# The scale of the SSD norm kept in DRAM and applied when six groups' tiles are loaded back

## The chip, the cores and the metric

The kernel runs on one core of a Trainium2 chip. Its time is device microseconds; of several executions the median counts. A profile is one further execution, recorded by the hardware. The engines are named PE (TensorE, matmuls), DVE (VectorE), ACT (ScalarE), POOL (GpSimd) and SP (SyncE), which here issues every DMA on one queue, in program order.

## What is computed

One encoder layer for two requests of 256 tokens (together 512 columns), width 1024, all in float32. What matters here is the middle part: three branches are made from the same projection, gated, added and projected. Branch B is the state-space scan (SSD) in 8 groups of 256 channels, whose output passes a gate and an RMS norm by group. Cut to these lines:

```
u = rms_norm(x, mix_norm);  proj = u @ w_in          # q, k, v, z, xbc, dt, gate_logits
o_na  = neighborhood_attention(q_na, k_na, v_na, na_rpb)
y_ssd = (y_fwd + y_bwd + ssd_d * xs).reshape(bsz, t, D_INNER) * silu(z)
o_ssd = grouped_rms_norm(y_ssd, ssd_norm, SSD_GROUPS)  # rms over the 256 channels of a group
o_mem = memory_attention(q_m, k_m, v_m)
merged = g_na * (o_na @ w_br_na) + g_ssd * (o_ssd @ w_br_ssd) + g_mem * (o_mem @ w_br_mem)
x = x + merged @ w_out
```

The norm of a group multiplies each channel by its own weight (`ssd_norm`) and each token by one over the root of the mean square of the group's 256 channels in that token.

## The kernel before

**Layout and precision.** Activations lie with channels on the 128 partitions and the 512 tokens along the row, so a tile is 128x512. Each operand of a large product is split into a high and a low part; a product of two is three matmuls (L543 `uh,wh`, L544 `ul,wh`, L545 `uh,wl`). One call of `unit` makes one 128x512 output in a PSUM bank from eight input tiles: 24 matmuls. Such units, one after the other through the whole program, are most of what PE does.

**Weights.** `fetch` (L288) loads weights into a ring of nine buffers `wr`; `ahead` splits them two units before their use, the high part by a copy on ACT (`wh`, L320), the low part by a subtraction on DVE (`wl`, L234).

**Order.** `run` goes through a fixed plan of slots. A slot is one unit, and after it `evacuate` moves the unit before from its bank and `step` advances side tasks, which are generators: each `next` runs a task to its next `yield`. At most three or four tasks are active; `later` queues one with the tasks that must be done before it. `require` steps the tasks without units until the named ones are done. A tile framework then gives out buffers, adds the waits and orders each engine's queue. Every engine runs its queue in order. Small DVE operations can be put on a chain (`link`), from which one is taken after each large DVE operation.

**The SSD stage.** For each of the eight groups the plan has eight slots (convolution inputs, gates, the other branch's products, two `z` products). Beside them runs `t_ssd(g)`: it transposes the group's two input tiles `xs` (on PE, `xT`, L1217), makes the products `CB`, and then goes through ten steps for its eight heads. For a head it loads a broadcast row (`rw<-scr_r`, L1202), makes two decay tiles `e` (ACT, then DVE: L245 and L234), and PE multiplies them (`y`, L1278). The result, times gate, is written over `xs`, which the profile calls `cv`; `yq` is its square. After the steps PE sums the squares over the channels (`sum`, L504), and a chain of eleven small DVE operations (L270 to L276) makes the inverse root `r`, four numbers on each of 128 partitions. For the multiplication `r` must become a row that is the same on all partitions. For g < KEEP (6) this goes through DRAM: store `scr_n` (L1299), broadcast load `rw` (L1302, 256 KB), two scalings `cv<-cv,half,rw` (L1311, in the profile under the helper's line L245), and stores of the two tiles to `scr_o` (L1313). For groups 6 and 7 it is made on chip: `dg` (DVE, L512), a matmul `R` (L521), then the same scaling with `R`, and the tiles stay.

**After it.** The gates' eight units for the SSD branch follow (their tanh, `tg`, is on ACT and frees their bank), then the branch's units, each of which reads all sixteen tiles split as `osh` and `osl`. `t_os(g)` makes these: it loads `or<-scr_o` (L1322) for groups 0 to 5 and splits (ACT `osh` L256, DVE `osl` L234). Groups 0 to 3 are queued with the first gate unit, groups 4 to 7 at the branch.

Of the kernel before, what the change touches and what calls it, by code (L numbers as in the profile page):

```python
# [10 lines left out]
ALU = mybir.AluOpType  # L11
# [167 lines left out]
KEEP, EARLY, PG, LEND = 6, 4, 54, 4  # L179
# [3 lines left out]
class Layer:  # L183
# [1021 lines left out]
    def t_ssd(self, g):  # L1205
# [3 lines left out]
        rw = {n: self.rows(g, *heads[n]) for n in range(2)}  # L1209
        xs = [self.o.pop(("cv", 2 * g + i)) for i in range(2)]  # L1210
        bm, cm = self.o.pop(("cv", 16 + g)), self.o.pop(("cv", 24 + g))
        xt = []
        for i in range(2):
            ps = self.bank("xT")
# [10 lines left out]
        for b in range(2):  # L1225
            ps = self.bank("CB")
# [41 lines left out]
        for n in range(10):  # L1268
            if n < 6:
                rw[n + 2] = self.rows(g, *heads[n + 2])  # L1270
            if n >= 3 and n % 2:
                i, b, _ = heads[n - 3]
# [12 lines left out]
            if n in (5, 9):  # L1285
                v = xs[i]
# [7 lines left out]
        self.tt(y[0], y[0], y[1], ALU.add)  # L1294
        r = self.rsqrt(self.rows_to_cols(y[0])[:, 0:4], 4, 1.0 / 1024)
        if g < KEEP:
            yield
            self.link(99)
            self.nc.sync.dma_start(out=self.scr_n[g].rearrange("t p -> p t"), in_=r)  # L1299
            ps = self.g(p="rw")  # L1300
            sn = self.scr_n
            self.nc.sync.dma_start(out=ps, in_=bass.AP(sn.tensor, sn.offset + g * 512, [[0, 128], [1, 512]]))  # L1302
            yield
            yield
        else:
            dg = self.spread(r)
            yield
            ps = self.spread_mm(dg)
        for i in range(2):
            v = xs[i]  # L1310
            self.stt(v, v, self.half[:, 2 * g + i:2 * g + i + 1], ps, ALU.mult, ALU.mult)  # L1311
            if g < KEEP:
                self.nc.sync.dma_start(out=self.scr_o[2 * g + i], in_=v)  # L1313
            else:
                self.oraw[2 * g + i] = v

    def t_os(self, g):
        for k in (2 * g, 2 * g + 1):
            t = self.oraw.pop(k, None)
            if t is None:  # L1320
                t = self.g(p="or")
                self.nc.sync.dma_start(out=t, in_=self.scr_o[k])  # L1322
            self.os[k] = self.split_tile(t, "os")
        return
        yield
# [90 lines left out]
```

## Time and profile before

| | us |
|---|---|
| median of 3 runs | 1781.8 |
| lowest and highest of them | 1779.09, 1783.22 |
| the profiled execution, its own time | 1783.05 |
| span of its instructions | 1781.2 |
| busy PE, DVE, ACT in it | 1750.0, 1230.8, 848.0 |
| mean granted TensorE clock | 0.995 of full |

The span is from the first to the last instruction; what the time has beside it, 1.85 us, lies around. Positions such as 1220.02 are microseconds from the span's start. The profile's waits give, for each engine, how long it was idle just before an instruction and what ended that.

### The profile page before, as it was taken

The numbers are of one execution on the slowest core, as the hardware profiler recorded it, in microseconds if no ns is written. First come the engines' busy times: TensorE is split into PE (matmuls) and PEld (weight loads), VectorE is DVE, ScalarE is ACT, GpSimd is POOL, SyncE is SP. The second block draws the span as 40 slices with busy tenths as digits, with TensorE's granted clock in tenths as the row PEclk, the third lists the DMA queues.
The fourth block names the chain that finished last, engine by engine and source line by source line (L and its number), as shares of the span: only waits on it lengthen the run. The fifth ranks groups of instructions, "written<-read, shape, count | busy, mean of one in ns | idle before, by whom it ended". The sixth has DMA issues, their size and how long they took to land.

```text
span 1781.2 us, 22578 instructions
## 1 busy us (share of the span) xinstructions
PE 1750.0 (98%) x8568; PEld 1426.1 (80%) x8568; DVE 1230.8 (69%) x2056; ACT 848.0 (48%) x1515; POOL 0.7 (0%) x5
## 2 busy tenths in 40 slices
PE   9999999999999999999999999998999999999999
PEld 7888888888788878788877777776788878888887
DVE  7676777875645467736878777987753697776775
ACT  6443444543324335533666565666632464444442
POOL 0000000000000000000000000000000000000000
PEclk9999999999999999999999999999999999999999
DMA  6134324542323132333333443446434324343331
GB/s 256 64 134 142 108 93 136 166 142 95 95 74 118 60 114 80 116 95 95 127 105 137 128 128 103 145 136 177 142 113 136 95 95 131 94 142 129 91 124 47
DMA packets 79708, 209.69 MB, mean 118 GB/s; under 512 B 11120, under 2 KB 19696, under 8 KB 79600
## 3 DMA queue, kind: packets, MB, share of 16 engines
q1 hardware_dynamic: 79600, 208.26, 36.7%
q8 instruction: 67, 1.10, 0.2%
q14 instruction: 41, 0.34, 0.1%
HBM read 198.64 MB, written 9.58 MB: 117 GB/s over the span
## 4 chain that ended last, share of the span: by engine, by line
PE 84%; DVE 7%; DMA 5%; issue 1%; ACT 1%; SPq 0%; DVEq 0%; ACTq 0%
PE ac L565 21%; PE m L543 9%; PE m L545 9%; PE m L544 9%; PE q L587 5%; PE q L589 5%; PE q L588 5%; PE d L544 4%; PE d L545 4%; PE d L543 4%; DMA scr_n<-y 3%; DVE cv L245 2%; DVE wl L234 2%; DMA rw<-scr_r 2%; PE y L1278 1%; DVE e L245 1%
## 5 line engine op out<-in xcount | busy, mean ns | idle before, releaser
L320 ACT CAST wh<-wr 128x1024 fp32r<-128x1024 f32 (+1 forms) x357 | 371.0, 1040 | 681.2 <-PE ac L565 166.8
L234 DVE TENSOR_TENSOR wl<-wr,wh 128x1024 fp32r<-128x1024 f32 (+1 forms) x357 | 431.4, 1209 | 270.5 <-ACT wh L320 265.3
L543 PE MATMUL m<-uh,wh 128*128 128x512 f32 (+1 forms) x584 | 236.3, 405 | 1.4 <-ACT tg L249 1.4
L565 PE MATMUL ac<-wh,sh 128*128 128x512 f32 (+1 forms) x616 | 229.3, 373 | 0.8 <-ACT wh L320 0.8
L545 PE MATMUL m<-uh,wl 128*128 128x512 f32 (+1 forms) x584 | 229.5, 393 | 0.0
L544 PE MATMUL m<-ul,wh 128*128 128x512 f32 (+1 forms) x584 | 229.4, 393 | 0.0
L565 PE MATMUL ac<-wl,sh 128*128 128x512 f32 (+1 forms) x616 | 228.1, 370 | 0.7 <-DVE wl L234 0.7
L565 PE MATMUL ac<-wh,sl 128*128 128x512 f32 (+1 forms) x616 | 228.1, 370 | 0.0
L543 PEld LDWEIGHTS m<-uh,wh 128*128 128x128 f32 (+1 forms) x584 | 110.2, 189 | 35.8 <-issue 8.4
L544 PE MATMUL d<-hl,wh 128*128 128x512 f32 x352 | 137.2, 390 | 0.7 <-DVE hl L234 0.7
L543 PE MATMUL d<-hh,wh 128*128 128x512 f32 x352 | 137.4, 390 | 0.5 <-ACT hh L256 0.5
L545 PE MATMUL d<-hh,wl 128*128 128x512 f32 x352 | 137.0, 389 | 0.0
L565 PEld LDWEIGHTS ac<-wh,sh 128*128 128x128 f32 x616 | 116.0, 188 | 21.0 <-ACT wh L320 1.7
L565 PEld LDWEIGHTS ac<-wl,sh 128*128 128x128 f32 x616 | 116.1, 189 | 20.7 <-DVE wl L234 1.2
L565 PEld LDWEIGHTS ac<-wh,sl 128*128 128x128 f32 x616 | 116.0, 188 | 19.6
L545 PEld LDWEIGHTS m<-uh,wl 128*128 128x128 f32 (+1 forms) x584 | 109.9, 188 | 26.0 <-issue 1.5
L544 PEld LDWEIGHTS m<-ul,wh 128*128 128x128 f32 (+1 forms) x584 | 110.2, 189 | 21.9
L249 ACT ACTIVATE e<-rw,lots 128x256 f32<-128x256 f32 (+1 forms) x256 | 97.8, 444 | 46.3 <-DMA rw<-scr_r 46.3
L245 DVE SCALAR_TENSOR_TENSOR x<-d,x 128x512 f32<-128x512 f32 x96 | 66.2, 690 | 77.1 <-PE d L545 76.8
L587 PE MATMUL q<-wh,uh 128*128 128x512 f32 x256 | 102.5, 400 | 0.0
L234 DVE TENSOR_TENSOR wr<-wr,wr 128x1024 f32<-128x1024 f32 x80 | 97.6, 1221 | 5.6 <-DMA wr<-in_w 4.3
L588 PE MATMUL q<-wh,ul 128*128 128x512 f32 x256 | 100.3, 392 | 0.0
(253 smaller groups left out, 2868.1 us busy)
## 6 DMA issues: line engine op xcount, KB each, us to landing
wr<-in_w SPq DMA_DIRECT2D x308, 512.0 KB
rw<-scr_r SPq DMA_DIRECT2D x64, 256.0 KB
nv<-scr_v SPq DMA_DIRECT2D x64, 64.0 KB
scr_o<-cv SPq DMA_DIRECT2D x12, 256.0 KB
or<-scr_o SPq DMA_DIRECT2D x12, 256.0 KB
wr<-in_w SPq DMA_DIRECT2D x9, 256.0 KB
x<-in_xT SPq DMA_DIRECT2D x8, 256.0 KB
mr<-in_memT SPq DMA_DIRECT2D x8, 256.0 KB
```

The lines of the kernel that those rows point to most:

```text
L234: self.V.tensor_tensor(out=out, in0=a, in1=b, op=op)
L245: self.V.scalar_tensor_tensor(out=out, in0=a, scalar=s, in1=b, op0=op0, op1=op1)
L249: self.S.activation(out=out, in_=x, func=f, **kw)
L320: self.S.copy(hi[:, :n], t[:, :n])
L543: self.T.matmul(ps[:m], wh[:, kk, :], xh, start=i == 0, stop=False)
L544: self.T.matmul(ps[:m], wh[:, kk, :], xl, start=False, stop=False)
L545: self.T.matmul(ps[:m], wl[:, kk, :], xh, start=False, stop=i == n - 1)
L565: go = lambda l, r, **f: self.T.matmul(ps, l, r, skip_group_check=True, **f)
L587: self.T.matmul(self.qb[t], xh, wh[:, kk, :], start=k == 0, stop=False)
L588: self.T.matmul(self.qb[t], xl, wh[:, kk, :], start=False, stop=False)
L589: self.T.matmul(self.qb[t], xh, wl[:, kk, :], start=False, stop=k == KD - 1)
L1278: T.matmul(yb[64 * hp:64 * hp + 64, b * 256:(b + 1) * 256], xt[i][:, (2 * b + st) * 128 + 64 * hp:(2 * b + st) * 128 + 64 * hp + 64], w[hp ...
```

## The change

The scale `r` of groups 0 to 5 stays in DRAM. `t_ssd` stores its two tiles unscaled to `scr_o` before the norm is made, then stores `r` to `scr_n` and ends, two `yield`s earlier than before. `t_os` loads `r` as a broadcast row together with the tiles and scales each tile after its load, ahead of the split. Groups 6 and 7 are as before. The number of DMAs and of DVE operations stays the same.

```
         if g < KEEP:
+            for i in range(2):
+                self.nc.sync.dma_start(out=self.scr_o[2 * g + i], in_=xs[i])
             yield
             self.link(99)
             self.nc.sync.dma_start(out=self.scr_n[g].rearrange("t p -> p t"), in_=r)
-            ps = self.g(p="rw")
-            sn = self.scr_n
-            self.nc.sync.dma_start(out=ps, in_=bass.AP(sn.tensor, sn.offset + g * 512, [[0, 128], [1, 512]]))
-            yield
-            yield
-        else:
-            dg = self.spread(r)
-            yield
-            ps = self.spread_mm(dg)
+            return
+        dg = self.spread(r)
+        yield
+        ps = self.spread_mm(dg)
         for i in range(2):
-            v = xs[i]
-            self.stt(v, v, self.half[:, 2 * g + i:2 * g + i + 1], ps, ALU.mult, ALU.mult)
-            if g < KEEP:
-                self.nc.sync.dma_start(out=self.scr_o[2 * g + i], in_=v)
-            else:
-                self.oraw[2 * g + i] = v
+            self.scale_o(g, i, xs[i], ps)
+            self.oraw[2 * g + i] = xs[i]
+
+    def scale_o(self, g, i, v, r):
+        self.stt(v, v, self.half[:, 2 * g + i:2 * g + i + 1], r, ALU.mult, ALU.mult)
 
     def t_os(self, g):
-        for k in (2 * g, 2 * g + 1):
+        if g < KEEP:
+            r, sn = self.g(p="rw"), self.scr_n
+            self.nc.sync.dma_start(out=r, in_=bass.AP(sn.tensor, sn.offset + g * 512, [[0, 128], [1, 512]]))
+        for i in range(2):
+            k = 2 * g + i
             t = self.oraw.pop(k, None)
             if t is None:
                 t = self.g(p="or")
                 self.nc.sync.dma_start(out=t, in_=self.scr_o[k])
+                self.scale_o(g, i, t, r)
             self.os[k] = self.split_tile(t, "os")
```

What this does to the engines' queues is shown at three places. Numbers behind a name tell one buffer from another; they differ between the kernels.

**First piece: PE, the end of group 7,** just ahead of the SSD branch's first unit. In the kernel before, `sum` stands inside a gate unit `m_11108`, whose matmuls are the three lines of a product:

```order
L543 MATMUL m_11108<-uh_3254,wh_11000 128x512
L544 MATMUL m_11108<-ul_3255,wh_11000 128x512
L545 MATMUL m_11108<-uh_3254,wl_11001 128x512
L543 MATMUL m_11108<-uh_3261,wh_11000 128x512
L504 MATMUL sum_11077<-consts,yq_10932 128x1 x4
L544 MATMUL m_11108<-ul_3262,wh_11000 128x512
L545 MATMUL m_11108<-uh_3261,wl_11001 128x512
L543 MATMUL m_11108<-uh_3320,wh_11000 128x512
```

and `R` eleven matmuls later:

```order
L543 MATMUL m_11108<-uh_3381,wh_11000 128x512
L544 MATMUL m_11108<-ul_3382,wh_11000 128x512
L545 MATMUL m_11108<-uh_3381,wl_11001 128x512
L521 MATMUL R_11101<-dg_11085,consts 128x128 x4
L543 MATMUL m_11108<-uh_3388,wh_11000 128x512
L544 MATMUL m_11108<-ul_3389,wh_11000 128x512
```

In the changed kernel the last `y` of group 7 is followed by the same two:

```order
L545 MATMUL m_11035<-uh_3381,wl_10930 128x512
L543 MATMUL m_11035<-uh_3388,wh_10929 128x512
L544 MATMUL m_11035<-ul_3389,wh_10929 128x512
L1278 MATMUL y_10972<-e_10982,xt_10546 64x256
L1278 MATMUL y_10972<-e_10965,xt_10546 64x256
L1278 MATMUL y_10972<-e_10982,xt_10546 64x256
L545 MATMUL m_11035<-uh_3388,wl_10930 128x512
L504 MATMUL sum_11069<-consts,yq_10924 128x1 x4
L521 MATMUL R_11093<-dg_11077,consts 128x128 x4
L543 MATMUL m_11100<-uh_3206,wh_10992 128x512
L544 MATMUL m_11100<-ul_3207,wh_10992 128x512
L545 MATMUL m_11100<-uh_3206,wl_10993 128x512
```

The last `y` stands six matmuls later in its unit than before (seven of that unit follow it there, one here), and `sum` and `R` have moved up ahead of the next unit, next to each other.

**Second piece: SP, the norm of group 0.** Before (`cv_7052` and `cv_7125` are the group's tiles, `rw<-scr_r` loads those of the group behind it):

```order
L1299 DMA scr_n<-y_7844 128x4x1
L1302 DMA rw_7913<-scr_n 128x512
L1202 DMA rw_7915<-scr_r 128x512
L1202 DMA rw_7967<-scr_r 128x512
L288 DMA wr_8049<-in_w 128x1024
L1202 DMA rw_8026<-scr_r 128x512
L1313 DMA scr_o<-cv_7052 128x512
L1313 DMA scr_o<-cv_7125 128x512
L288 DMA wr_8113<-in_w 128x1024
```

and in the changed kernel:

```order
L1298 DMA scr_o<-cv_7125 128x512
L1202 DMA rw_7783<-scr_r 128x512
L1202 DMA rw_7848<-scr_r 128x512
L1202 DMA rw_7915<-scr_r 128x512
L1202 DMA rw_7967<-scr_r 128x512
L288 DMA wr_7935<-in_w 128x1024
L1202 DMA rw_8022<-scr_r 128x512
L288 DMA wr_7983<-in_w 128x1024
L1301 DMA scr_n<-y_7844 128x4x1
L288 DMA wr_8045<-in_w 128x1024
L288 DMA wr_8109<-in_w 128x1024
```

The load behind the store is gone, the loads `rw<-scr_r` that stood behind it are ahead of it, and the tile's store too.

**Third piece: ACT and DVE at the place of the first.** ACT before:

```order
L320 CAST wh_11046<-wr_10577 128x1024
L256 CAST osh_10824<-or_10822 128x512
L256 CAST osh_10831<-or_10829 128x512
L320 CAST wh_11111<-wr_10579 128x1024
L249 ACTIVATE tg_10895<-m_10717 128x512
L249 ACTIVATE tg_10965<-m_10864 128x512
L249 ACTIVATE tg_11028<-m_10934 128x512
L249 ACTIVATE yq_11041<-cv_10473 128x512
L249 ACTIVATE tg_11074<-m_10997 128x512
```

and in the changed kernel:

```order
L320 CAST wh_11038<-wr_10553 128x1024
L256 CAST osh_10802<-or_10798 128x512
L320 CAST wh_11103<-wr_10555 128x1024
L256 CAST osh_10810<-or_10807 128x512
L249 ACTIVATE yq_11033<-cv_10453 128x512
L256 CAST osh_10819<-or_10816 128x512
L256 CAST osh_10826<-or_10823 128x512
L249 ACTIVATE tg_10887<-m_10693 128x512
L249 ACTIVATE tg_10957<-m_10856 128x512
```

`tg`, the tanh whose unit's bank the next unit takes, stands ahead of `yq` before; now it stands behind two copies `osh`, and these need scaled tiles `or`. DVE, from the last `y` to the scaling by `R`, before:

```order
L245 SCALAR_TENSOR_TENSOR cv_10473<-cv_10473,half,y_10980 128x512
L234 TENSOR_TENSOR cv_10473<-cv_10473,zt_10677 128x512
L234 TENSOR_TENSOR osl_10832<-or_10829,osh_10831 128x512
L234 TENSOR_TENSOR wl_11112<-wr_10579,wh_11111 128x1024
L234 TENSOR_TENSOR yq_10932<-yq_10932,yq_11041 128x512
L270 TENSOR_SCALAR v_11082<-sum_11077 128x4
```

and in the changed kernel:

```order
L245 SCALAR_TENSOR_TENSOR cv_10453<-cv_10453,half,y_10972 128x512
L245 SCALAR_TENSOR_TENSOR or_10807<-or_10807,half,rw_10796 128x512
L234 TENSOR_TENSOR cv_10453<-cv_10453,zt_10653 128x512
L234 TENSOR_TENSOR wl_11104<-wr_10555,wh_11103 128x1024
L234 TENSOR_TENSOR osl_10811<-or_10807,osh_10810 128x512
L234 TENSOR_TENSOR yq_10924<-yq_10924,yq_11033 128x512
L270 TENSOR_SCALAR v_11074<-sum_11069 128x4
```

A scaling of `or` has come between the result of `y` and the add of the squares `yq`, and `wl` and `osl` have changed places. Farther on in the changed kernel, the end of the inverse root:

```order
L275 SCALAR_TENSOR_TENSOR t_11076<-t_11076,v_11074 128x4
L276 SCALAR_TENSOR_TENSOR y_11075<-t_11076,y_11075 128x4
L234 TENSOR_TENSOR osl_10820<-or_10816,osh_10819 128x512
L512 TENSOR_SCALAR dg_11077<-consts,y_11075 128x128 x4
L245 SCALAR_TENSOR_TENSOR cv_10340<-cv_10340,half,R_11093 128x512
L245 SCALAR_TENSOR_TENSOR or_10823<-or_10823,half,rw_10814 128x512
L245 SCALAR_TENSOR_TENSOR cv_10453<-cv_10453,half,R_11093 128x512
L234 TENSOR_TENSOR osl_10827<-or_10823,osh_10826 128x512
```

Here an `osl` stands ahead of `dg`, and the scaling of the second `or` between the two by `R`; a scaling of `or` stands inside the inverse root as well. Before, nothing stands there.

## Rows read from the trace of the kernel before

**Rows 1.** The page's first part: the span, then each engine's busy time, its share of the span, and its instructions.

```profile
span 1781.2 us, 22578 instructions
PE 1750.0 (98%) x8568; PEld 1426.1 (80%) x8568; DVE 1230.8 (69%) x2056; ACT 848.0 (48%) x1515; POOL 0.7 (0%) x5
```

**Rows 2.** The waits of PE over the whole span: the waiting instruction, what it waited for, us in total, times, the longest.

```profile
PE y L1278 <- DVE e L234: 7.6, 5, 5.2
PE xT L1217 <- DVE cv L245: 7.0, 4, 2.2
...
PE m L543 <- ACT tg L249: 1.4, 1, 1.4
```

**Rows 3.** The same view of SP's DMA queue, of DVE and of ACT, the rows that touch the change.

```profile
SPq L1302 <- DMA scr_n<-y: 48.8, 6, 8.8
...
DVE cv L245 <- DMA rw<-scr_n: 34.2, 6, 6.8
...
ACT e L249 <- DMA rw<-scr_r: 46.3, 6, 8.6
...
ACT osh L256 <- DMA or<-scr_o: 4.3, 4, 1.4
```

**Rows 4.** The timeline of SP's queue in group 5: start, duration, line, transfer.

```profile
1210.38 0.38 SPq L1299 DMA_DIRECT2D scr_n<-y  x1
...
1220.02 0.33 SPq L1302 DMA_DIRECT2D rw<-scr_n  x1
```

**Rows 5.** The timelines of DVE, ACT and PE at the same place; in brackets the idle time before and what ended it.

```profile
1224.07 0.75 DVE L245 SCALAR_TENSOR_TENSOR cv<-cv,half,rw 128x512 f32<-128x512 f32 x1 [5.61 <-DMA rw<-scr_n]
...
1226.04 1.49 ACT L249 ACTIVATE e<-rw,lots 128x256 f32<-128x256 f32 x4 [7.70 <-DMA rw<-scr_r]
...
1219.75 0.40 PE L545 MATMUL m<-uh,wl 128*128 128x512 f32 x1
1225.31 1.94 PE L1278 MATMUL y<-e,xt 128*64 128x256 f32 x6 [5.16 <-DVE e L234]
```

**Rows 6.** Busy time by stretch: from and to, length, then busy time and count of PE, PEld, DVE, ACT, POOL, the granted clock, the DMA engines' share and GB/s. First periods of the SSD groups, from one store of `scr_n` to the next; then two stretches behind waits; last the end of the stage.

```profile
930.80:985.10 54.30, 53.68 (x249) 41.10 (x248) 45.52 (x95) 35.41 (x74) 0.00 (x0) 1.00 0.39 131
985.10:1041.80 56.70, 54.76 (x250) 42.26 (x249) 45.57 (x96) 35.47 (x74) 0.00 (x0) 0.97 0.41 126
...
1154.90:1210.40 55.50, 53.89 (x250) 41.12 (x249) 45.58 (x95) 35.47 (x74) 0.00 (x0) 1.00 0.42 128
...
1002.70:1006.00 3.30, 3.30 (x11) 2.73 (x11) 3.30 (x8) 2.38 (x5) 0.00 (x0) 0.50 0.26 99
...
1225.30:1231.20 5.90, 5.89 (x16) 3.93 (x17) 5.90 (x12) 5.08 (x12) 0.00 (x0) 0.50 1.04 395
...
1262.00:1285.00 23.00, 23.00 (x108) 15.47 (x107) 18.89 (x41) 15.63 (x36) 0.00 (x0) 1.00 0.54 182
```

**Rows 7.** The timeline of PE at the end of group 7. Instructions of one form that follow each other are one row.

```profile
1287.10 0.50 PE L543 MATMUL m<-uh,wh 128*128 128x512 f32 x1 [1.40 <-ACT tg L249]
...
1287.90 0.40 PE L543 MATMUL m<-uh,wh 128*128 128x512 f32 x1
...
1289.27 0.39 PE L543 MATMUL m<-uh,wh 128*128 128x512 f32 x1
1289.50 0.95 PE L504 MATMUL sum<-consts,yq 128*128 128x1 f32 x8
1290.31 0.48 PE L544 MATMUL m<-ul,wh 128*128 128x512 f32 x1
...
1292.67 0.39 PE L545 MATMUL m<-uh,wl 128*128 128x512 f32 x1
1293.09 1.13 PE L521 MATMUL R<-dg,consts 128*128 128x128 f32 x8
1293.98 0.47 PE L543 MATMUL m<-uh,wh 128*128 128x512 f32 x1
```

**Rows 8.** The timeline of DVE at the same place, the first `y` result to the scaling by `R`.

```profile
1283.91 0.75 DVE L245 SCALAR_TENSOR_TENSOR cv<-cv,half,y 128x512 f32<-128x512 f32 x1 [2.53 <-PE y L1278]
1284.69 0.69 DVE L234 TENSOR_TENSOR cv<-cv,zt 128x512 f32<-128x512 f32 x1
1285.30 0.69 DVE L234 TENSOR_TENSOR osl<-or,osh 128x512 fp32r<-128x512 f32 x1
1286.59 1.23 DVE L234 TENSOR_TENSOR wl<-wr,wh 128x1024 fp32r<-128x1024 f32 x1 [0.60 <-ACT wh L320]
1288.58 0.69 DVE L234 TENSOR_TENSOR yq<-yq,yq 128x512 f32<-128x512 f32 x1 [0.77 <-ACT yq L249]
1290.48 0.16 DVE L270 TENSOR_SCALAR v<-sum 128x4 f32<-128x4 f32 x1 [1.21 <-PE sum L504]
...
1292.66 0.88 DVE L512 TENSOR_SCALAR dg<-consts,y 128x128 f32<-128x128 f32 x4
1294.26 1.41 DVE L245 SCALAR_TENSOR_TENSOR cv<-cv,half,R 128x512 f32<-128x512 f32 x2 [0.73 <-PE R L521]
```

**Rows 9.** Groups of instructions by line, engine, operation and form: count, busy us, mean ns of one, idle time before.

```profile
L245 DVE SCALAR_TENSOR_TENSOR cv<-cv,half,rw 128x512 f32<-128x512 f32 x12 | 8.6, 750 | 34.2 <-DMA rw<-scr_n 34.2
...
L249 ACT ACTIVATE tg<-m 128x512 f32<-128x512 f32 x24 | 13.8, 591 | 0.0
L256 ACT CAST osh<-or 128x512 fp32r<-128x512 f32 x12 | 7.3, 616 | 4.3 <-DMA or<-scr_o 4.3
```

## The prediction

> **What bounds the kernel now.** I read the page's engine shares first: PE is busy 1750.0 of 1781.2 us [rows 1]. PE takes its instructions in order, so only what leaves a hole in PE, or lowers its clock, costs time, and a change elsewhere is worth what it does to those holes. Then PE's waits [rows 2]: of few that there are, the first two belong to the SSD stage, `y` behind DVE's `e` 7.6 us and `xT` behind DVE's `cv` 7.0 us. They name DVE, which is only 69% busy [rows 1], so something holds DVE up. The waits of the other engines [rows 3] tell what: DVE's scaling of `cv` waits 34.2 us in six times for the load `rw<-scr_n`; SP, which issues every DMA in order, waits 48.8 us in six times for the store `scr_n<-y` to land before it can issue that load; and ACT waits 46.3 us for `rw<-scr_r`, loads of the next group that stand in SP's queue behind it. The last group with this store shows the chain on one clock [rows 4, 5]: the store is issued at 1210.38 and the load only at 1220.02; DVE starts its scaling at 1224.07 after 5.61 us idle, ACT starts at 1226.04 after 7.70, and PE, which left its last matmul at 1219.75, starts `y` at 1225.31. So PE's 14.6 us in this stage are the round trip through DRAM, passed on by two in-order queues.
>
> **The change, part by part: what it takes away.** In groups 0 to 5 nothing in the SSD stage reads `scr_n` any more: the load and the scaling go to `t_os`. The store stays and nothing waits for it for a long time, so SP goes on at once to `wr` loads, while the next `rw<-scr_r` loads stand ahead of it (second piece of order). The terms:
> - PE's waits: 7.6 + 7.0 = 14.6 us [rows 2].
> - A hole costs more than its idle time, since the pipeline drains: from 1219.75 to 1225.31 [rows 5] is 5.56 us, 5.33 above the pitch of 0.23 between `m` matmuls (six from 1287.90 to 1289.27, [rows 7]), against 5.16 shown as idle. Nine holes at 0.2 make 1.8 us.
> - Clock: after two of the holes the granted clock is 0.50, the 1.2 GHz level, for 3.30 and 5.90 us with PE busy throughout [rows 6]. Half of each is lost: 1.65 + 2.95 = 4.6 us.
>
> The gain is 14.6 + 1.8 + 4.6 = 21.0 us. A check from other rows: the first group's period, with one hole of 0.6, is 54.3 us; the four that follow last 1210.4 - 985.1 = 225.3 us, 8.1 above four times that [rows 6]. They hold the 7.0 of `xT`, no more of `y` than the first, and the 1.65 of the clock, 8.65 in all: the holes do carry through to the end. What the freed stage does with its time must not be a new hole: DVE is busy 45.5 of 54 to 57 us a group [rows 6], and loses the two scalings (1.5 us at 750 ns, [rows 9]), so it has 8 us a group to spare. The `scr_o` stores are issued earlier, behind a DVE row that is due anyway; I cost them at nothing, covered by the three to eight `wr` buffers ahead, and if that cover were gone each could delay a weight load by the wait for its tile. Bounds of the gain: 14.6 (waits alone, the clock falling elsewhere) and 21.6 (0.3 a hole).
>
> **What it adds.** Twelve scalings `or<-or,half,rw` (0.75 us each, 9.0 us on DVE) and six loads go to the stretch before the SSD branch. DVE is busy there 18.89 of 23.00 us [rows 6], so the five scalings that fall ahead of the last `y` (3.5 us at 0.70) about fill it. That is DVE time, not PE time. But the tail's order on PE changes, and this is the dear part (first piece of order). Before, seventeen matmuls stand between the last `y` and `sum`, and eleven more ahead of `R`; they cover DVE's chain. Now `sum` and `R` follow the last `y` with one matmul between, back to back, so PE stands through the whole of it. And the next unit's first matmul waits for a tanh `tg` to free its bank (it does so before, 1.40 us, [rows 2, 7]), which on ACT now stands behind two `osh` copies, the second of which wants a scaling that stands behind `R` (third piece).
>
> The chain from the start of DVE's `cv<-cv,half,y`, durations from [rows 8, 9]: 0.78 to the next start, scaling of `or` 0.70, `cv,zt` 0.61, `wl` 1.23, `osl` 0.61, `yq` add 0.69: 4.6. From the add's end (1288.58 + 0.69) to `v` at 1290.48: 1.21, makes 5.8. The eleven small operations to `dg`, 1290.48 to 1292.66: 2.18, makes 8.0. A scaling and an `osl` set among them: 1.4, makes 9.4. `dg` to the scaling by `R`, 1292.66 to 1294.26: 1.60, makes 11.0. That scaling 0.70, the second `or` 0.75, `osh` 0.62, `tg` 0.59: 13.7 us. The chain starts in before's time at 1283.91 plus six matmuls by which the last `y` now stands later (1.4) plus 0.5 for a DVE that is full: 1285.8. So the next unit starts at 1299.5 where it started at 1287.10 [rows 7]: 12.4 us later. `sum` and `R` are then behind it already; before, they took 0.58 (1289.50 to 1290.31, less a pitch) and 1.08 (1292.67 to 1293.98, less one): 1.66. That leaves 10.7. After a hole of 5.16 us the clock cost 2.95; I take 3.0 for this one too. Loss 13.7 us. Its bounds: 8 (no clock loss, the slip nothing, `tg` not held by the last `osh`) and 20 (3 us of slip on a full DVE, 6.8 us at half clock, `sum` and `R` at the low clock too). The four scalings of groups 4 and 5, later still, stand ahead of `os` tiles that the branch's first unit reads last; I cost them at nothing, from 0 to 3 us.
>
> **Sum.** 13.7 - 21.0 = -7.3 us on the profiled execution's 1783.05, so 1775.7. That execution is 1.25 above the median of 1781.8, so for the median 1774.5.
>
> The price of a clock that has fallen is the one term that could be read otherwise. Rows 6 show 3.30 and 5.90 us at half clock behind holes of 1.94 and 5.16 us. The Trainium skill, page "TensorE: Matmul & The Clock Gate", section "HAM oscillation — how this bites in real kernels", reports about 1.67 us throttled behind each wait of its kernel, half of it lost. By that figure, as an estimate, two stretches give back 1.7 in place of 4.6 and the new one costs 0.8 in place of 3.0: -6.6 in place of -7.3. The measured stretches decide.
>
> **Rivals.**
> (a) *The tail is hidden and the gain comes whole.* For it: in before DVE's chain there is covered and PE waits 1.40. Against: PE's order leaves one matmul of cover. It gives 1783.05 - 21.0 - 1.25 = 1760.8. Chance 0.14.
> (b) *The tail eats the gain.* The clock falls as often as before, only elsewhere, so the gain is the waits, 14.6, and the tail costs 13.7 or a little more: 1779 to 1784. The 9.4 us of the chain ahead of `dg` are on a DVE that has no slack, which speaks for it. Chance 0.16.
> (c) *Slower: the scalings stand on DVE waiting for their loads.* Before, only ACT's copy waits for `or<-scr_o`, 4.3 us in four times [rows 3], while DVE goes on. Now DVE, in order, waits for `or` and `rw`, and behind it stand the `e` that PE's `y` need. From its issue at 1220.02 a load is used at 1224.07: 4.05 us [rows 4, 5]. Four of the eight tiles exposed by that are 16.2 us, less the 4.1 idle on DVE (23.00 - 18.89): 12.1 more on PE, net +4.8, 1786.6. It decides from a tail loss of 21.0 + 3.6 = 24.6 us on, three to four loads wholly exposed. Against it: the loads are issued well ahead where buffers are free. Chance 0.12.
> (d) *The holes stay.* PE's `y` waits name DVE's `e`, not the load; if DVE is late there by its own work, 2.4 of them remain and the result is 1777. It lies inside my forecast's own range.
>
> **The numbers.** My forecast (net -3.6 to -15) has 0.58; its own range is 1766 to 1778. Bounds of both terms, -21.6 + 8 and -14.6 + 20, reach from 1768 to 1787. 0.2% of this time is 3.6 us, about what a measurement can tell from no change, so faster means under 1778.2 and slower over 1785.4. Faster is my forecast and (a), 0.72; same is (b), 0.16; slower is (c), 0.12. The range 1763 to 1783 leaves out most of (a) below and (c) above, 2 in 10.
>
> **What would show it.** The gain is right if DVE has no wait for `rw<-scr_n` in the SSD groups, SP none of 8 us there, PE's `xT` waits are gone, the group period is 53 to 54 us, and the clock stays at 1.00 to the end of group 5. The tail is right if PE waits for `sum`, `R` and `m` in a row for some 10 us just ahead of the SSD branch, with the clock at 0.50 behind it. I am wrong if DVE's waits for `or<-scr_o` or the moved `rw<-scr_n` reach 10 us, if PE's `y` waits for `e` grow in groups 6 and 7, or if the group period stays at 56.

## The result and the profile after

The changed kernel takes 1768.5 us, median of 4 runs (1767.54 to 1769.75), against 1782.5 for the kernel before in the same comparison (4 runs, 1779.09 to 1784.56). The ratio is 0.9924, interval 0.9907 to 0.9941, so 10.5 to 16.6 us are saved. The forecast was faster, 1774.5 in a range of 1763 to 1783: the direction and the mechanism held, and the saving came out at 14 us where 7 were forecast. The profiled execution took 1768.09 us with a span of 1766.3.

The page's first part of the changed kernel, to be read against [rows 1]:

```profile
span 1766.3 us, 22623 instructions
...
PE 1741.1 (99%) x8568; PEld 1425.2 (81%) x8568; DVE 1232.2 (70%) x2056; ACT 847.3 (48%) x1515; POOL 0.7 (0%) x5
```

PE's busy time has fallen by 8.9 us with the same number of instructions, so part of what was lost before had counted as busy. PE's waits over the whole span, against [rows 2]:

```profile
PE sum L504 <- DVE yq L234: 4.1, 1, 4.1
PE R L521 <- DVE dg L512: 3.7, 1, 3.7
...
PE m L543 <- ACT tg L249: 2.7, 1, 2.7
...
PE y L1278 <- DVE e L234: 0.7, 1, 0.7
```

`xT` is off the list and `y` is down from 7.6 to 0.7. At one place the waits for `sum` and `R` are new, and the one for `tg` has grown from 1.4 to 2.7. Of DVE's and ACT's waits for these loads, against [rows 3], none for `scr_n` is left, and two remain:

```profile
DVE or L245 <- DMA or<-scr_o: 4.5, 2, 2.3
...
ACT e L249 <- DMA rw<-scr_r: 1.1, 1, 1.1
```

The periods of the SSD groups, from one store of `scr_n` to the next, and three later stretches (from and to, length, then busy time and count of PE, PEld, DVE, ACT, POOL, granted clock, DMA share, GB/s), against [rows 6]:

```profile
930.90:983.10 52.20, 52.20 (x250) 40.91 (x249) 44.64 (x93) 35.27 (x75) 0.00 (x0) 1.00 0.42 131
983.10:1035.30 52.20, 52.20 (x250) 40.90 (x249) 44.63 (x93) 35.29 (x75) 0.00 (x0) 1.00 0.53 131
...
1139.70:1191.90 52.20, 52.20 (x250) 40.91 (x249) 44.63 (x93) 35.27 (x75) 0.00 (x0) 1.00 0.45 132
...
1262.80:1272.70 9.90, 3.63 (x16) 3.28 (x16) 6.30 (x21) 1.73 (x4) 0.00 (x0) 0.50 0.36 127
1272.80:1276.30 3.50, 3.50 (x8) 2.77 (x9) 0.13 (x1) 1.86 (x4) 0.00 (x0) 0.50 0.00 0
```

A group now takes 52.2 us with PE busy all of it, where it took 54.3 to 56.7. The clock is at 1.00 through the SSD groups and at 0.50 (the 1.2 GHz level) from 1262.8 to 1276.3, behind the last `y` and a wait of 4.1 us. That place, on PE, DVE and ACT of the changed kernel, against [rows 7, 8]:

```profile
1257.08 1.08 PE L1278 MATMUL y<-e,xt 128*64 128x256 f32 x6
1258.09 0.50 PE L545 MATMUL m<-uh,wl 128*128 128x512 f32 x1
1262.69 1.70 PE L504 MATMUL sum<-consts,yq 128*128 128x1 f32 x8 [4.10 <-DVE yq L234]
1268.06 2.05 PE L521 MATMUL R<-dg,consts 128*128 128x128 f32 x8 [3.68 <-DVE dg L512]
1272.76 0.80 PE L543 MATMUL m<-uh,wh 128*128 128x512 f32 x1 [2.65 <-ACT tg L249]
...
1258.19 0.75 DVE L245 SCALAR_TENSOR_TENSOR cv<-cv,half,y 128x512 f32<-128x512 f32 x1 [1.58 <-PE y L1278]
...
1261.86 0.68 DVE L234 TENSOR_TENSOR yq<-yq,yq 128x512 f32<-128x512 f32 x1
1264.42 0.16 DVE L270 TENSOR_SCALAR v<-sum 128x4 f32<-128x4 f32 x1 [1.88 <-PE sum L504]
...
1267.64 0.87 DVE L512 TENSOR_SCALAR dg<-consts,y 128x128 f32<-128x128 f32 x4
1270.15 0.75 DVE L245 SCALAR_TENSOR_TENSOR cv<-cv,half,R 128x512 f32<-128x512 f32 x1 [1.64 <-PE R L521]
1270.81 0.75 DVE L245 SCALAR_TENSOR_TENSOR or<-or,half,rw 128x512 f32<-128x512 f32 x1
...
1271.59 0.62 ACT L256 CAST osh<-or 128x512 fp32r<-128x512 f32 x1 [4.68 <-DVE or L245]
1272.12 2.54 ACT L249 ACTIVATE tg<-m 128x512 f32<-128x512 f32 x5
```

This is the chain that was forecast, link by link: `y`, the square's add, `sum`, the inverse root, `dg`, `R`, the second scaling of `or`, `osh`, `tg`, and only then the next unit.

How far the changed kernel is ahead at each place follows from equal matmuls. The last run of `y` in the kernel before:

```profile
1282.79 1.08 PE L1278 MATMUL y<-e,xt 128*64 128x256 f32 x6
```

Its start, plus 1.4 for the six matmuls by which it now stands later, less 1257.08, is 27.1 us. The first `m` of the next unit: 1287.10 [rows 7] less 1272.76, 14.3 us. So the SSD groups gave 27 and the tail took back 13.

### The profile page after: what moved, and what is told of

Read it like the earlier page. It is cut to its first block, busy times and chain, and to the rows that moved or that the text cites. A ratio compares the mean times of both kernels' runs of the same rounds, so it can differ in the third digit from the quotient of the medians.

```text
span 1766.3 us, 22623 instructions
## 1 busy us (share of the span) xinstructions
PE 1741.1 (99%) x8568; PEld 1425.2 (81%) x8568; DVE 1232.2 (70%) x2056; ACT 847.3 (48%) x1515; POOL 0.7 (0%) x5
## 4 chain that ended last, share of the span: by engine, by line
PE 95%; DVE 3%; DMA 1%; issue 0%; ACT 0%; DVEq 0%; SPq 0%; ACTq 0%
PE ac L565 20%; PE m L543 12%; PE m L544 12%; PE m L545 12%; PE q L587 5%; PE q L589 5%; PE q L588 5%; PE d L544 5%; PE d L545 5%; PE d L543 5%; PE y L1278 2%; PE hT L690 1%; PE CB L1228 1%; DVE wl L234 1%; PE amo L875 1%; PE am L847 1%
## 5 line engine op out<-in xcount | busy, mean ns | idle before, releaser
L589 PE MATMUL q<-wl,uh 128*128 128x512 f32 x256 | 100.6, 393 | 0.0
```

The lines of the kernel that those rows point to most:

```text
L589: self.T.matmul(self.qb[t], xh, wl[:, kk, :], start=False, stop=k == KD - 1)
```

## Experiments

All times are medians of 4 runs, and ratios are to the kernel before on the same chip in the same job.

**1. Is it the round trip?** Kernel before, the load reads elsewhere:

```
             ps = self.g(p="rw")
-            sn = self.scr_n
+            sn = self.scr_r
```

> The kernel before, but the broadcast load behind the store of the scale reads a row of the decay scratch that was written long ago, so it does not wait for the store to land; the store stays, and so do the load's size, both scalings, the stores of the tiles and every yield. The scaling is by wrong numbers: the norm's scale is left out of groups 0 to 5. My theory (the round trip through DRAM is the gain): SP's 8 us waits and DVE's 34 us are gone, PE's waits for xT and y go, the tail stays covered, and the time is 24 to 28 us below the kernel before, near 1756. Rival (the gain comes from taking twelve scalings off DVE and two steps off each group's task): both are still there, so it lies within 6 us of before.

Measured: 1755.39 us, ratio 0.9852 (0.9837 to 0.9866), 26 us less. In its SSD groups PE has no wait and DVE none for `rw`, while the scalings and yields are where they were. The rival falls; the whole of the gain is there without moving the scalings. The scheduler does order PE otherwise here: its `m` matmuls are broken by runs of `y` 34 times, as in the changed kernel, and not 40 as in the kernel before. So the 26 us hold the waits and this difference of order together (run 8 prices the breaks). One of the four small `y` holes of the kernel before and two of its four `xT` holes, on PE; this kernel has none of them:

```profile
953.44 1.05 PE L1278 MATMUL y<-e,xt 128*64 128x256 f32 x6 [0.62 <-DVE e L234]
...
1002.59 1.05 PE L1217 MATMUL xT<-consts,cv 128*128 128x128 f32 x4 [1.94 <-DVE cv L245]
...
1115.90 0.63 PE L1217 MATMUL xT<-consts,cv 128*128 128x128 f32 x4 [2.21 <-DVE cv L245]
```

The `xT` at 1002.59 ran at a granted clock of 0.50 [rows 6], those at 1115.90 at 1.00.

**2. Do the two yields matter?** Changed kernel:

```
             self.nc.sync.dma_start(out=self.scr_n[g].rearrange("t p -> p t"), in_=r)
+            yield
+            yield
             return
```

> The changed kernel with the two yields of before put back behind the store of the scale, so that each group's task ends as late as before. My theory (the gain is the wait, the tail is made by the moved scalings): as the changed kernel, 1768.5 within 2 us, with the same waits for sum, R and m of 4, 4 and 3 us. Rival (ending two steps earlier makes the gain, or makes the tail): either the SSD periods grow back and it is 5 us or more slower, or the tail's waits go and it is 10 us faster.

Measured: 1768.43 us, ratio 0.9926 (0.9910 to 0.9943), and the same waits for `sum`, `R` and `tg` (4.1, 3.7, 2.6). Ending the tasks earlier makes neither the gain nor the loss.

**3. Is the tail made by the moved scalings?** Changed kernel, `t_os` without them:

```
-        if g < KEEP:
-            r, sn = self.g(p="rw"), self.scr_n
-            self.nc.sync.dma_start(out=r, in_=bass.AP(...))
...
-                self.scale_o(g, i, t, r)
```

> The changed kernel without the loads of the scale and the twelve scalings where the tiles are loaded back: the norm's scale is left out of groups 0 to 5. My theory (they alone lead to sum and R standing bare): the tail is covered as before, PE's waits for sum and R are below 1 us, and the time is 12 to 14 us below the changed kernel, near 1755. Rival (the tail's order comes from tasks that end earlier): the waits of 4, 4 and 3 us stay and the time is within 3 us of 1768.5.

Measured: 1756.08 us, ratio 0.9855 (0.9840 to 0.9869), 12.5 below the changed kernel. PE's only wait from 900 to 1330 us is that for `tg` of before:

```profile
PE m L543 <- ACT tg L249: 1.4, 1, 1.4
```

With the loads and the scalings out, `sum` and `R` stand in PE's queue as they did before, apart and covered. So the loss goes with them: with them in, the scheduler puts `sum` and `R` elsewhere. What they cost as work alone is not told apart; three scalings of `or`, some 0.7 us each, stand in the changed kernel's chain of 14.6 us.

**4. Fewer of them ahead of the branch.** Changed kernel:

```
-KEEP, EARLY, PG, LEND = 6, 4, 54, 4
+KEEP, EARLY, PG, LEND = 6, 2, 54, 4
```

> The changed kernel with only groups 0 and 1 loaded back, scaled and split during the gates, and 2 to 7 at the branch (the constant EARLY 2 in place of 4). In its order on PE, 22 rows stand between the last y and sum and 13 more ahead of R. My theory (the loss is the bare chain): the waits for sum, R and m go, unless the branch's first unit has to wait for the eight scalings that are later now; 8 to 13 us below the changed kernel, 1755 to 1760. Rival (the eight scalings at the branch cost what they saved): PE waits there for osh or osl by 5 to 10 us and the time stays within 4 us of 1768.5.

Measured: 1760.58 us, ratio 0.9882 (0.9868 to 0.9897), 8 below the changed kernel, just outside the range given. PE's waits from 1230 to 1330 us:

```profile
PE m L543 <- ACT osh L256: 2.0, 2, 1.1
PE m L543 <- ACT wh L320: 1.4, 1, 1.4
PE m L545 <- DVE wl L234: 0.4, 1, 0.4
```

The bare chain is gone and the branch's first units wait a little for their tiles. Both theories hold in part: 12 to 13 us saved at the one place and the 1.4 for `tg` with it, and by the start times of the matmuls some 6 paid at the other, of which the waits listed are 3.8.

**5. The scale on chip for all groups.** Kernel before:

```
-        if g < KEEP:
-            yield
...
-            yield
-        else:
-            dg = self.spread(r)
-            yield
-            ps = self.spread_mm(dg)
+        dg = self.spread(r)
+        yield
+        ps = self.spread_mm(dg)
```

> The kernel before with the scale of all eight groups made a row on chip, as it does for groups 6 and 7 (dg on DVE, the matmul R on PE, the scaling by R, then the stores of the tiles for groups 0 to 5): the same results, no scr_n at all. It keeps 40 runs of y matmuls between m matmuls, as before has; the changed kernel has 34. My theory (holes as they are listed, and beside them about 0.7 us for each run of y that breaks the m matmuls once more): 1781.5 less 27.5, plus six breaks or 4, plus six R of 1.1 us or 6.5: 1764 to 1765, and in the trace 29 plain runs of y between m, against 23. Rival (the breaks cost nothing, all of the 27 is the holes): 1760 to 1761, with a break at its own matmuls' time.

Measured: 1765.77 us, ratio 0.9907 (0.9893 to 0.9922). The number is near the forecast, but for another reason. From 920 us on, where the kernel before has 29 plain runs of `y` between `m`, this one has 24 runs with `y` and no `CB`, 7 of them with `R`: the count of 40 that I expected took a run broken by `R` for one broken by `m`. PE's timeline at the first of these `R`:

```profile
933.61 0.38 PE L521 MATMUL R<-dg,consts 128*128 128x128 f32 x2
933.92 0.65 PE L1278 MATMUL y<-e,xt 128*64 128x256 f32 x2
934.50 0.94 PE L521 MATMUL R<-dg,consts 128*128 128x128 f32 x6
935.37 1.08 PE L1278 MATMUL y<-e,xt 128*64 128x256 f32 x6
```

`R` costs here not the 1.1 us of [rows 7] but breaks a run of `y` in two as well. Against run 1 the time is 10 us longer, or 1.7 for each of the six. So the run shows again that no round trip means no hole, and says nothing of its own on breaks.

**6. Which queue passes the wait on?** Kernel before:

```
             self.nc.sync.dma_start(out=self.scr_n[g].rearrange("t p -> p t"), in_=r)
+            yield
+            yield
             ps = self.g(p="rw")
...
             yield
-            yield
```

> The kernel before with one more yield, two of the three between the store of the scale and the emission of its load; in SP's order the load still stands directly behind the store, the scaling comes one step later. It tells apart which in-order queue passes the round trip on. Theory A (DVE's queue: the scaling stands on it waiting): DVE's waits for rw<-scr_n fall to below 5 us and so do PE's holes, time near 1757, although SP goes on waiting 8 us six times. Theory B (SP's queue: the next group's rw<-scr_r stand behind the blocked load): ACT's waits for rw<-scr_r stay at 30 to 50 us, PE keeps waits for y, time 1766 to 1776. I expect B, with xT's waits gone and some of y's left.

Measured: 1755.42 us, ratio 0.9846 (0.9830 to 0.9863). I expected B and got A's time. SP, DVE and ACT in this kernel, against [rows 3]:

```profile
SPq L1304 <- DMA scr_n<-y: 44.2, 6, 8.1
...
DVE cv L245 <- DMA rw<-scr_n: 6.2, 6, 1.3
...
ACT e L249 <- DMA rw<-scr_r: 0.4, 1, 0.4
```

SP waits for the store as long as before (44.2 against 48.8 us), and PE has no wait in the SSD groups at all. The time is that of run 1, in which SP does not wait, so SP's blocked queue costs nothing here by itself: what cost was that DVE and ACT stood for what comes through it. In this kernel four `rw<-scr_r` stand ahead of the store:

```profile
1178.50 1.85 SPq L1202 DMA_DIRECT2D rw<-scr_r  x4
...
1193.76 0.38 SPq L1299 DMA_DIRECT2D scr_n<-y  x1
1196.53 0.33 SPq L288 DMA_DIRECT2D wr<-in_w  x1
1203.07 0.33 SPq L1304 DMA_DIRECT2D rw<-scr_n  x1
1203.44 0.42 SPq L1202 DMA_DIRECT2D rw<-scr_r  x1
```

Both the scaling and the use of the row loads have moved away from the block, so whether DVE's wait or ACT's was the dearer is not told apart.

**7. Scaled a group later.** Kernel before; `t_ssd` of the next group loads and scales:

```
         for n in range(10):
+            if late and n == 4:
+                lr, sn = self.g(p="rw"), self.scr_n
+                self.nc.sync.dma_start(out=lr, in_=bass.AP(...))
+            if late and n == 6:
+                for i in range(2):
+                    self.scale_o(late[0], i, late[1][i], lr)
+                    self.nc.sync.dma_start(out=self.scr_o[2 * late[0] + i], in_=late[1][i])
```

The stores go with the scaling; the load, the scalings and their two yields leave the group's own task, and a group's `t_os` waits for the next group's task.

> The kernel before, but a group's scale is loaded, and its tiles scaled and stored, in the steps 4 and 6 of the next group's task; on SP some ten DMAs stand between the store and the load. The same results. The twelve scalings stay in the SSD groups and t_os is as before. My theory (the round trip is the gain, the scalings among the gates are the loss): both PE's holes in the SSD stage and the tail's waits are gone, 1755 to 1758, 11 to 13 us below the changed kernel. Rival (the scalings and late stores fill DVE in the SSD groups, or the tiles come late for the gates' loads): waits of PE for e or for osh come back, 1760 or more.

Measured: 1756.14 us, ratio 0.9852 (0.9837 to 0.9867). As my theory had it: SP has no wait for the store any more, PE none but the 1.4 for `tg`. It is no faster than run 6, in which SP still waits.

**8. What does a break cost?** Kernel of run 6:

```
-                for st in range(2):
-                    for hp in range(2):
-                        T.matmul(yb[...], xt[i][...], w[hp][0][...], start=st == 0, stop=st == 1)
+                half = lambda st, i=i, b=b, w=w, yb=yb: [T.matmul(yb[...], ...) for hp in range(2)]
+                half(0)
+                if n in (5, 9):
+                    half(1)
+            elif n in (4, 8):
+                half(1)
```

> The kernel of the run with the scaling a step later, with the same y matmuls, but in every other step the second half of the four is issued one step later; so PE's m matmuls are broken by y 47 times by its order, in place of 34. Results as the reference. My theory for the part of the gain that the listed waits don't hold (the kernel before breaks them 40 times, the changed one 34): each break costs about 0.65 us beside its own matmuls, 13 more make 8.5: 1763 to 1765, with no waits of PE in the SSD stage. Rival (a break costs nothing, the 27 us were all holes): 1755 to 1757.5.

Measured: 1759.49 us, ratio 0.9865 (0.9847 to 0.9883); run 6 had 1755.42 and 0.9846, and the intervals overlap, so of the times alone neither number is settled. The trace has the price. A run of `y`, from PE's timeline of the kernel before, of the changed kernel, and of this one, with the `m` on both sides:

```profile
938.03 0.39 PE L545 MATMUL m<-onh,wl 128*128 128x512 f32 x1
938.35 0.65 PE L1278 MATMUL y<-e,xt 128*64 128x256 f32 x2
938.93 0.50 PE L543 MATMUL m<-uh,wh 128*128 128x512 f32 x1
...
939.50 0.40 PE L545 MATMUL m<-uh,wl 128*128 128x512 f32 x1
939.82 1.08 PE L1278 MATMUL y<-e,xt 128*64 128x256 f32 x6
940.83 0.50 PE L543 MATMUL m<-uh,wh 128*128 128x512 f32 x1
```

```profile
937.59 0.39 PE L545 MATMUL m<-onh,wl 128*128 128x512 f32 x1
937.91 1.08 PE L1278 MATMUL y<-e,xt 128*64 128x256 f32 x8
938.92 0.50 PE L543 MATMUL m<-uh,wh 128*128 128x512 f32 x1
```

```profile
933.72 0.39 PE L545 MATMUL m<-uh,wl 128*128 128x512 f32 x1
934.04 0.65 PE L1277 MATMUL y<-e,xt 128*64 128x256 f32 x4
934.62 0.50 PE L543 MATMUL m<-on,wh 128*128 128x512 f32 x1
```

From `m` to `m`, less the pitch of 0.23: 0.67 us for a run of two, 0.67 for four, 1.10 for six and for eight. Split into two and six, eight cost 1.77, or 0.67 more; split into four and four 1.34, or 0.24 more. The first `m` behind each run is followed after 0.34 us and not 0.23, so each run more costs another 0.11. Both theories fail on their number for this kernel: thirteen more runs, most of them even halves, cost 3.5 us from `m` to `m` and 1.4 behind them, not 8.5 and not nothing; PE's wait of 1.4 for `tg` is gone here, so that the whole is some 3.4. For the kernel before, whose six more runs are the uneven kind, the 0.67 each stands.

## Why the prediction was right, and what was mis-sized

- **The bound and the mechanism** held: the holes in PE came from the round trip and went with it (runs 1 and 3). DVE has no wait for `rw<-scr_n` in the changed kernel, the clock stays at 1.00 through the SSD groups, and the three waits of the tail stand in a row, 10.5 us in all, with the clock at 0.50 from the end of the first, much as foretold.
- **The loss** was forecast at 13.7 us; the places above give 13 (27 ahead, then 14.3, and 14.9 in the span), and taking the scalings out gave 12.5 (run 3). The chain from `cv<-cv,half,y` to the next unit took 14.57 us against 13.7, the steps being: to the end of the square's add 4.35 (4.6 forecast), to `v` 6.23 (5.8), to `dg` 9.45 (9.4), to the scaling by `R` 11.96 (11.0), to `m` 14.57. What is over is the clock: `sum` and `R` ran at half of it, 1.70 and 2.05 us in place of 0.95 and 1.13. The `m` matmuls behind the chain lost 1.8 us to it, where I took 3.0.
- **The gain was mis-sized**: 21.0 forecast, 27 measured, and that is nearly the whole of the miss. It lies outside the bounds that I gave it, 14.6 to 21.6 (the upper one is 21.9 by its own terms); the net of 14 us is near the edge of the 3.6 to 15 that I gave it. From the start times of all PE matmuls of this stretch in the kernel before and in run 1, less the pitch, it divides so.
  - `xT`: 8.1 us where 7.0 of idle was listed. 0.3 of it is four `xT` at half clock (run 1), so a hole costs 0.2 above its idle time, as I took it.
  - The `y` hole of 5.2: 6.1, of which 0.85 is its six `y` at half clock (1.94 us in place of 1.08), so that hole costs 0.1 above its idle time.
  - The four `y` holes of 0.6, 2.4 together: 4.9, twice their idle time, where I took 0.2 each.
  - The clock: 3.1 on the `m`. With the shares of `xT` and `y` it makes 4.3, against 4.6 forecast, so this term held.
  - Four `sum`: 0.7, at a granted clock of 1.00; what held them is not shown.
  - And 4.4 that I had no term for, 4.0 from `m` to `m` and 0.4 on the `m` behind: the kernel before breaks its `m` matmuls once more in each of six groups, by two and six `y` where the changed kernel has eight in one run (run 8). That was in the order of the two kernels, and I read the order only where the change moved something that I knew of. Why the scheduler breaks them there is not shown.
- **The check that I made by the periods** hid this: it compared four groups with a first one that itself holds a hole and a break. The base is 52.2 us, not 54.3.
- **Two in-order queues pass the wait on**, I wrote, and costed SP's block as part of it. Run 6 shows that SP's block, kept almost whole, costs nothing once what is needed soon stands ahead of it.
- **The throttled time.** From the end of the tail's first wait the clock is at 0.50 for 13.5 us, of which PE works some 7. The figure of 1.67 us behind each wait, from the Trainium skill's page "TensorE: Matmul & The Clock Gate" (section "HAM oscillation — how this bites in real kernels"), makes 5.0 for three waits, as an estimate, and is too small here; the measurement decides.
- **Rivals**: (a) fell by the three waits; (b) by the gain; (c) by the waits for the loads, DVE's for `or<-scr_o` are 4.5 us in all, in two; (d) by PE's `y` at 0.7.

The best version is neither kernel: the kernel before with one more step between the store and the scaling (run 6) takes 1755.4 us, 13 below the change, and leaves nothing out; run 7 is level with it.

## What to carry over

A wait that an in-order engine passes on is mended by giving the answer time to come, one step of other work between request and use; moving the use far away can cost more where it lands. Before a piece of work is moved, read the whole order of the engine that sets the time, not only at the places that the change names: here the scheduler moved two groups of short matmuls out of their cover at one end, and joined runs of short matmuls at the other. Cost a hole by the starts on both sides, not by its idle time.

## What was not expected of the hardware

- A run of short `y` matmuls between long ones costs by its break as much as by its number: 0.67 us for two or for four, 1.10 for six or for eight.
- SP stood for 44 us in six waits (run 6) and the kernel lost nothing by it: 1755.4 us against 1755.4 in run 1 and 1756.1 in run 7, where it does not wait.
- At the end of a wait of 4.1 us the granted clock fell to 0.50, and it stayed there from 1262.8 to 1276.3, through the waits of 3.7 and 2.7 us that followed and 3.5 us beyond. In the kernel before, it had fallen behind a wait of 1.94 us, and not behind one of 2.21.
